# Grouped queries' root on GpSimd, the last heads' sums added through a 0/1 column, weight transfers queued at their buffer's due time

## The chip, the cores and the metric

One core of a Trainium2 chip runs the whole kernel. The metric is device time in microseconds (us): the median of the runs, 1585.17 for the kernel before (three runs, 1583.2 to 1587.08). Engines are called PE (TensorE matmuls), PEld (its weight loads), DVE (VectorE), ACT (ScalarE), POOL (GpSimd) and SP (SyncE, which only issues transfers here).

## The reference

Two layers of an encoder trunk over 512 tokens of width 1024, all in float32:

```python
h = rms_norm(x, attn_norm_g[l])
proj = h @ w_in[l]
c_q, c_kv, k_rope, gq, gk, gv, pool_in, gate_logits = split_columns(proj, IN_SIZES)
o_mla = mla_branch(c_q, c_kv, k_rope, ...)      # 8 heads, low-rank q and kv
o_gqa = gqa_branch(gq, gk, gv, ...)             # 8 query heads, 2 key heads, 64 wide
o_pool = pool_branch(pool_in, pool_w[l], pool_scale[l])
gates = sigmoid(gate_logits)                    # one per branch and channel
merged = sum(gate * (o @ w_branch) for the three branches)
x = x + merged @ w_out[l]
x = x + (silu(u_gate) * u_val) @ ffn_w_down[l]  # u: depthwise conv of rms_norm(x) @ ffn_w_up
```

In the grouped branch each of the 8 query heads is scaled by one over the root of its mean square plus 1e-6. For 512 tokens and 8 heads that is 128 x 32 numbers on the chip.

## The kernel before, in words

Float32 products are made of three matmuls of split operands (`mm3`, L382): each weight tile and each activation is cut into a rounded part and a remainder. The weights stream through a pool of three raw buffers (`rawp`, `RAW = 3`), each 1024 columns wide as a rule and filled by one transfer on SP (`w_dma`, L326). A buffer holds about two pieces of up to 512 columns. `w_split` (L333) cuts a piece: ACT writes the rounded part `wh`, then POOL or DVE subtracts it to give `wl`; `pick` decides which. Pieces are cut `LA = 3` ahead of the matmul that uses them.

The order on every engine is written by a planner inside the kernel: a `Clock` keeps an estimated time for each engine, `chain` queues the steps of a tile's way through the engines at their estimated times, and every PSUM bank has an estimated time at which it is free. Matmuls are emitted one after another, and what is due by the estimate is emitted ahead of them. The hardware then runs each engine's list in that order and waits on semaphores; an engine that waits holds up all that stands behind it.

A layer runs in this order. The normed input is multiplied with the latent columns, the pooled channels (four groups), the grouped queries (banks `AV`, `AV`, `mi`, `ST`) and the grouped keys and values; in the middle of the last stands the pooled branch's own product (`pool_product`). It uses the same four banks as the queries, and each bank is free again when DVE has made the remainder `opl` of that bank. Then come the gates of branch 2, whose first two take the `AV` banks, and the attention of the grouped heads.

The root of the grouped queries is stepped by hand: `gq_mean` scales and adds epsilon, `guess` makes a first value from the bits, three Newton steps follow, and `gq_token` multiplies with the token's own factor. All of it works on `ssr`, 128 x 32. `rsqrt_steps` (L440) makes these steps; without an engine given it puts all of them on DVE, nine instructions in three Newton steps. Four multiplications `gq_norm` on POOL follow, and the queries are then turned by PE (L379) or through DRAM.

Attention (`attention`) writes a list of steps for eight heads with positions `PLAN`: scores for the maximum (`s_max`, bank `S`), scores for the probabilities (`probs`, banks `ST`, `ST`, `mi`), products with the values (`av_hi`, `av_lo`), and a last product that adds a remainder (`av_rest`). The tiles `ph`, `pl` and `vt` carry the rounded probabilities, their remainder and that last sum. Between these steps a `Filler` puts units of other matmuls (gates, the branch products, the making of the latent heads' q, k, v): as many as the position asks for, and up to `SLACK = 35` more when the planner believes the step would wait. What is left of the filler when the last step is out goes behind it; the filler of the next attention starts after that. The latent heads' values leave their bank `acc` by a cast and four DVE subtractions (`vm`).

At a head pair's end (`o_out`, L1311) the two halves `oraw` and the row `osum` of sums have been copied from PSUM. Rows 0 and 64 of `osum` hold the sum of probabilities; the other rows hold remainders that have to be added to `oraw`. So, after a transpose and a reciprocal have taken what they need, `add` sets rows 0 and 64 to zero by two POOL memsets and adds the tiles: on POOL, and for head 7 on DVE.

The lines that matter: `w_ahead` (L357) queues weight transfers, `rsqrt_steps` (L440), `gq_mean` and `gq_token` in `layer`, `add` in `o_out`, and the memsets at the start (L1565).

Of the kernel before, what the change touches and what calls it, by code (L numbers as in the profile page):

```python
# [18 lines left out]
P = 128  # L19
T = 512  # L20
# [112 lines left out]
class Clock:  # L133
# [10 lines left out]
    def at(self, dt, fn):  # L144
        heapq.heappush(self.heap, (self.now + dt, self.n, fn))
        self.n += 1
# [24 lines left out]
    def done(self, *key):  # L171
        self.ready[key] = self.fin + self.SEM
# [90 lines left out]
def trunk(ctx: ExitStack, tc: tile.TileContext, x, w, prm, gb, cst, out):  # L263
# [62 lines left out]
    def w_dma():  # L326
        i = st["dma"]
        t = slot("raw") if i < KC else rawp.tile([P, 1024], F32, tag="raw", name=f"raw{i}")
        SY.dma_start(t[:, :swidth[i]], w[int(soff[i]):int(soff[i + 1])].rearrange("(p c) -> p c", p=P))
        raws[i] = t  # L330
        st["dma"] += 1

    def w_split():  # L333
        j = st["split"]
        sl, off, wd = pieces[j]
        r = raws[sl][:, off:off + wd]
        hi = hlp.tile([P, T], F32R, tag="wh", name=f"wh{j}")
        lo = hlp.tile([P, T], F32R, tag="wl", name=f"wl{j}")
        ck.fin = ck.now
        if j == 0:  # L340
            V.tensor_copy(hi[:, :wd], r)
        else:
            A.activation(hi[:, :wd], r, AF.Copy)
        e = V if j < KC + 3 else pick(W_BIAS, ck.fin + ck.SEM)
        ck.free[e.kind] = max(ck.free.get(e.kind, 0.0), ck.fin + ck.SEM)
        e.tensor_tensor(lo[:, :wd], r, f(hi[:, :wd]), ALU.subtract)
        done("w", j)
        halves[j] = (hi, lo)
        st["split"] += 1

    def pick(bias, t=0.0):

# [1 line left out]
        dve, pool = (max(t, ck.free.get(e, 0.0)) for e in ("DVE", "Pool"))  # L354
        return V if dve + 0.61 + bias < pool + 1.18 else G

    def w_ahead(j):  # L357
        while True:
            sj = st["split"]
            done = pieces[sj][0] if sj < len(pieces) else len(swidth)  # L360
            while st["dma"] < min(len(swidth), done + RAW):
                w_dma()
            if sj > min(j, len(pieces) - 1):
                return
            w_split()

    def wnext():
# [26 lines left out]
    xsp = dp.tile([KC, P, T], F32, tag="xsp", name="xsp")  # L394
    ident = C[:, C_ID:C_ID + P]
    mhalf = cp.tile([P, 1], F32, tag="mhalf", name="mhalf")
    eps = cp.tile([P, 1], F32, tag="eps", name="eps")


    MQ, MK = [[cp.tile([P, 4, 4, 96], F32, tag=f"{n}{g}", name=f"{n}{g}") for g in range(2)] for n in ("MQ", "MK")]  # L400
# [39 lines left out]
    def rsqrt_steps(a, n, key, eng=None):  # L440

        if n == 8:
            return [lambda: G.tensor_tensor(a, a, bc(mhalf, [P, 8]), ALU.pow), lambda: done(*key)]
        y = small("y0", [P, 32])[:, :n]
        t = small("yt", [P, 32])[:, :n]

        def newton(to):
            if eng:
                eng.tensor_tensor(t, y, a, ALU.mult)
                eng.tensor_tensor(t, t, y, ALU.mult)  # L450
                eng.tensor_scalar(t, t, -0.5, 1.5, ALU.mult, ALU.add)
                eng.tensor_tensor(to, t, y, ALU.mult)
                return
            V.tensor_tensor(t, y, a, ALU.mult)
            V.scalar_tensor_tensor(t, t, -0.5, y, ALU.mult, ALU.mult)
            V.scalar_tensor_tensor(to, t, 1.5, y, ALU.add, ALU.mult)

        def guess():
            V.tensor_scalar(y.bitcast(I32), a.bitcast(I32), -0.5, RSQRT_BITS, ALU.mult, ALU.add)

        def go():
            guess()
            for to in (y, y, a):
                newton(to)

        if eng:
            return [guess, *[lambda to=to: newton(to) for to in (y, y, a)], lambda: done(*key)]
        return [go, lambda: done(*key)]

    def norm_begin(gen, sq):  # L470

# [45 lines left out]
    def bc(ap, shape):  # L517
        return ap.to_broadcast(shape)
# [26 lines left out]
    def layer(l, sq, xsrc):  # L545
# [226 lines left out]
            chain(add, lambda: done("gqr", l, b), after=ck.fin - ck.now)  # L772

        def gq_mean():
            V.scalar_tensor_tensor(ssr[:, 0:32], ssr[:, 0:32], 1.0 / 64, bc(eps, [P, 32]), ALU.mult, ALU.add)

        def gq_token():
            s_ = ssr[:, 0:32].rearrange("p (b h) -> p b h", b=4)
            V.tensor_tensor(s_, s_, bc(nrm["rt"].unsqueeze(2), [P, 4, 8]), ALU.mult)

        def gq_norm(b):
            o = gqo[b][:, :T].rearrange("p (h f) -> p h f", f=64)
# [2 lines left out]

        chain(*[lambda b=b: gq_square(b) for b in range(4)])
        chain(*[lambda b=b: gq_rope(b) for b in range(4)])
        chain(([("gqs", l, b) for b in range(4)], gq_mean), *rsqrt_steps(ssr[:, 0:32], 32, ("ssr", l)), gq_token,
              *[([("gqr", l, b), ("gkn", l)], lambda b=b: gq_norm(b)) for b in range(4)])

        opool = {}
# [344 lines left out]
        def attention(kind, fill, okey, odst):  # L1136
# [174 lines left out]
            def o_out(h):  # L1311
                s = hs.pop(h)
                if h % 2 == 0:
                    ot[:] = [slot("oraw"), slot("osum")]
                raw, sums = ot
                js = slice(64 * (h % 2), 64 * (h % 2) + 64)

                def in_order(o, src):
                    if not gqa or h > 1:
                        o = o.rearrange("p (b i t) -> p i b t", b=4, i=4)  # L1320
                        src = src.rearrange("p (i b t) -> p i b t", b=4, i=4)
                    A.activation(o, src, AF.Copy)

                def copies():
                    in_order(sums[js, :T], s["av"][64:128])
                    in_order(raw[js, :T], s["av"][0:64])
                    free("AV")

                def add():

                    for j in (0, 64):
                        G.memset(sums[j:j + 1, :T], 0.0)
                    (V if h == 7 else G).tensor_tensor(raw[:, :T], raw[:, :T], sums[:, :T], ALU.add)

                steps = [copies]
                if h % 2 == 1:
                    oh, ol = slot("oh", F32R), slot("ol", F32R)
                    odst[h // 2] = (oh, ol)

                    turned, inv = slot("otr"), small("oinv", [P, 16])  # L1340
                    steps += [lambda: V.transpose(turned[:, :T], sums[:, :T]),
                              lambda: V.reciprocal(inv, turned[:, :T].rearrange("p (b f) -> p b f", f=32)[:, :, 0])]
                    steps += [add, lambda: (A.activation(inv[32:64], inv[0:32], AF.Copy),
                                            A.activation(inv[96:128], inv[64:96], AF.Copy))]
                    steps += [lambda: V.transpose(sums[:, :T].rearrange("p (b f) -> p b f", f=32),
                                                  bc(inv.unsqueeze(2), [P, 16, 32]))]
                    steps += [lambda: (V if h == 7 else G).tensor_tensor(raw[:, :T], raw[:, :T], sums[:, :T], ALU.mult),
                              *split(oh[:, :T], ol[:, :T], raw[:, :T], eng=V if h == 7 else G),
                              lambda: done(okey, l, h // 2)]
                chain(*steps)  # L1350
# [211 lines left out]
    V.memset(warm, 0.0)  # L1562
    A.activation(warm, warm, AF.Exp)
    V.memset(mhalf, -0.5)
    V.memset(eps, EPS)  # L1565
    G.memset(f(unit), 0.0)
    G.memset(f(unit[:, 0:1]), 1.0)
    idle = ps("mi")
# [169 lines left out]
```

## Time and profile before

| what | value |
|---|---|
| median of the runs (range) | 1585.17 us (1583.2 to 1587.08) |
| the profiled execution's own span, first instruction to last | 1584.1 us |
| mean granted PE clock | 0.997 |
| PE busy | 1567.5 us, 99% |
| DVE, ACT, POOL busy | 949.1, 789.7, 1022.0 us |
| weight transfers of 512 KB on SP | 230, median 3.4 us to landing |

The span is within the range of the timed runs and 1.07 us under their median. A view of waits gives, for an engine, the line that waited, who released it, the total in us, how often, and the longest. A timeline gives the start, the busy time, engine, line, operation, output and inputs, and in brackets the idle time before it with its releaser. A table by stretches gives the busy time of each engine with its number of instructions, the granted clock, the share of the transfer engines and GB/s. A row on a tile gives the least, the median and the largest duration in ns.

### The profile page before, as it was taken

Reading aid. Unit: us, or ns where it says so; the run is one execution under the profiler, and the core shown is the slowest. Engines: PE = TensorE matmul, PEld = TensorE weight load, DVE = VectorE, ACT = ScalarE, POOL = GpSimd, SP = SyncE. Lnnn points to the kernel's source line nnn. Section 1 sums busy time; section 2 is a strip of 40 time slices with the busy share of each in tenths; the row PEclk is TensorE's granted clock in tenths of the full one; section 3 lists DMA queues with packets and bytes.
Section 4 is the critical chain, followed back from the end, with each engine's and each line's share of the span. In section 5 each row is a group of like instructions: output and inputs, shape, how many; then the busy total and the mean of one; then the engine's idle time right before and its main releaser. Section 6 shows DMA issues by size and latency. Waiting matters only on the chain.

```text
span 1584.1 us, 20341 instructions
## 1 busy us (share of the span) xinstructions
PE 1567.5 (99%) x7098; PEld 1310.2 (83%) x7098; DVE 949.1 (60%) x1351; ACT 789.7 (50%) x1436; POOL 1022.0 (65%) x889
## 2 busy tenths in 40 slices
PE   9989999999999999999999999999999999999999
PEld 8878878888888888888898888788888888888888
DVE  6767876875257776720047788678652677777000
ACT  5547766763444444432244677666634444444221
POOL 3854886754667667654568658868546676666542
PEclk9999999999999999999999999999999999999999
DMA  6422224323323232233335322343242233223331
GB/s 206 125 92 81 77 82 146 117 67 120 120 80 107 93 107 93 94 120 107 113 107 129 103 72 74 101 142 103 67 146 93 83 108 103 94 93 106 120 113 47
DMA packets 86070, 164.43 MB, mean 104 GB/s; under 512 B 25040, under 2 KB 47056, under 8 KB 85968
## 3 DMA queue, kind: packets, MB, share of 16 engines
q1 hardware_dynamic: 81072, 162.93, 32.5%
q8 instruction: 56, 0.92, 0.2%
q10 hardware_dynamic: 4896, 0.21, 0.2%
q14 instruction: 46, 0.38, 0.1%
HBM read 149.41 MB, written 13.63 MB: 103 GB/s over the span
## 4 chain that ended last, share of the span: by engine, by line
PE 90%; DVE 4%; POOL 2%; DMA 1%; ACT 1%; issue 1%; SPq 0%; ACTq 0%; POOLq 0%; DVEq 0%
PE ps_acc L375 40%; PE ps_AV L375 22%; PE ps_ST L375 21%; PE ps_S L375 3%; PE ps_mi L375 3%; DVE XM L231 1%; DMA raw<-w 1%; POOL wl L231 1%; DVE mgl L231 1%; ACT mgh L224 1%; DVE gt L235 0%; POOL win L231 0%; POOL tabm L231 0%; POOL fac L231 0%; DMA tf<-dl 0%
## 5 line engine op out<-in xcount | busy, mean ns | idle before, releaser
L231 POOL TENSOR_TENSOR wl<-raw,wh 128x512 fp32r<-128x512 f32 (+2 forms) x502 | 675.4, 1357 | 420.0 <-ACT wh L224 388.5
L224 ACT ACTIVATE wh<-raw 128x512 fp32r<-128x512 f32 (+3 forms) x521 | 308.8, 606 | 124.5 <-PE ps_ST L375 45.5
L235 DVE SCALAR_TENSOR_TENSOR a<-u,prm,a 128x511 f32<-128x511 f32 x176 | 241.6, 1375 | 90.8 <-ACT a L224 87.8
L375 PE MATMUL ps_acc<-HH,wh 128*128 128x512 f32 x592 | 232.2, 392 | 6.0 <-DVE vm L231 5.7
L375 PE MATMUL ps_acc<-HL,wh 128*128 128x512 f32 x592 | 231.8, 392 | 0.0
L375 PE MATMUL ps_acc<-HH,wl 128*128 128x512 f32 x592 | 231.8, 392 | 0.0
L375 PEld LDWEIGHTS ps_acc<-HH,wh 128*128 128x128 f32 x592 | 111.7, 189 | 29.1 <-issue 7.1
L375 PEld LDWEIGHTS ps_acc<-HH,wl 128*128 128x128 f32 x592 | 111.6, 188 | 23.9
L375 PEld LDWEIGHTS ps_acc<-HL,wh 128*128 128x128 f32 x592 | 111.6, 188 | 22.9
L375 PE MATMUL ps_AV<-HH,wh 128*128 128x512 f32 x288 | 113.7, 395 | 4.7 <-DVE ssr L231 4.2
L375 PE MATMUL ps_AV<-HL,wh 128*128 128x512 f32 x288 | 113.2, 393 | 0.0
L375 PE MATMUL ps_AV<-HH,wl 128*128 128x512 f32 x288 | 113.1, 393 | 0.0
L231 POOL TENSOR_TENSOR al<-a,ah 128x512 fp32r<-128x512 f32 x44 | 58.1, 1320 | 83.4 <-ACT ah L224 81.4
L239 DVE TENSOR_REDUCE nm<-ps_S 128x1 fp32r<-128x512 f32 x128 | 87.6, 684 | 33.0 <-PE ps_S L375 31.8
L375 PE MATMUL ps_ST<-HH,wh 128*128 128x512 f32 x240 | 93.5, 390 | 0.0
L375 PE MATMUL ps_ST<-HL,wh 128*128 128x512 f32 x240 | 93.4, 389 | 0.0
L375 PE MATMUL ps_ST<-HH,wl 128*128 128x512 f32 x240 | 93.4, 389 | 0.0
L224 ACT ACTIVATE ah<-a 128x512 fp32r<-128x512 f32 x44 | 27.8, 632 | 127.8 <-DVE a L231 127.8
L224 ACT ACTIVATE a<-u,prm 128x512 f32<-128x512 f32 x88 | 71.0, 809 | 24.8 <-DVE u L231 24.4
L224 ACT ACTIVATE a<-a 128x512 f32<-128x512 f32 x44 | 27.6, 632 | 103.4 <-DVE a L235 103.4
L224 ACT ACTIVATE HH<-XM,prm 128x512 fp32r<-128x512 f32 x32 | 23.1, 722 | 103.6 <-DVE XM L231 53.9
L224 ACT ACTIVATE ps_ST<-ps_ST 128x512 f32<-128x512 f32 x86 | 49.9, 581 | 49.3 <-PE ps_ST L375 49.3
(376 smaller groups left out, 3727.1 us busy)
## 6 DMA issues: line engine op xcount, KB each, us to landing
raw<-w SPq DMA_DIRECT2D x230, 512.0 KB, 3.4
raw<-w SPq DMA_DIRECT2D x14, 384.0 KB, 3.1
XM<-x SPq DMA_DIRECT2D x16, 256.0 KB, 3.6
dtq<-tr SPq DMA_DIRECT2D x16, 192.0 KB, 3.0
dtk<-tr SPq DMA_DIRECT2D x16, 192.0 KB, 3.6
tf<-dtq SPq DMA_DIRECT2D x48, 64.0 KB, 2.1
tf<-dtk SPq DMA_DIRECT2D x48, 64.0 KB, 2.3
xsp<-XM SPq DMA_DIRECT2D x8, 256.0 KB, 2.0
```

Of the source, the lines that this page charges most:

```text
L224: return self.eng.activation(out, in_, func, **k)
L231: return self.eng.tensor_tensor(out, *a)
L235: return self.eng.scalar_tensor_tensor(out, *a)
L239: return self.eng.tensor_reduce(out, in_, *a, **k)
L375: PE.matmul(o, lhsT=lhsT, rhs=rhs, start=start, stop=stop)
```

## The change

There are three edits. **The root:** `gq_mean`, the Newton steps and `gq_token` of the grouped queries go to POOL; only `guess` stays on DVE. A Newton step is now four POOL instructions in place of three on DVE, and the planner puts each step out by itself. **The sums:** for head 7, `add` no longer has POOL set rows 0 and 64 to zero: one DVE instruction multiplies `osum` with a column `keep` (1, with 0 in rows 0 and 64) and adds `oraw`. `keep` takes the place of `eps` and is made by three memsets at the start. **The transfers:** the transfer that refills a buffer was queued on SP in the same call that had split the last piece out of it; now it is queued when, by the planner's clock, that split is done. What is due before then goes ahead of it on SP.

```diff
@@ w_split
         st["split"] += 1
+        if j + 1 == len(pieces) or pieces[j + 1][0] > sl:
+            at(ck.fin - ck.now, lambda: w_until(sl + RAW))
...
+    def w_until(i):
+        while st["dma"] <= min(i, len(swidth) - 1):
+            w_dma()
+
     def w_ahead(j):
-        while True:
-            sj = st["split"]
-            done = pieces[sj][0] if sj < len(pieces) else len(swidth)
-            while st["dma"] < min(len(swidth), done + RAW):
-                w_dma()
-            if sj > min(j, len(pieces) - 1):
-                return
+        while st["split"] <= min(j, len(pieces) - 1):
+            w_until(pieces[st["split"]][0])
             w_split()
...
-    eps = cp.tile([P, 1], F32, tag="eps", name="eps")
+    keep = cp.tile([P, 1], F32, tag="keep", name="keep")
...
         def newton(to):
-            if eng:
-                eng.tensor_tensor(t, y, a, ALU.mult)
-                eng.tensor_tensor(t, t, y, ALU.mult)
-                eng.tensor_scalar(t, t, -0.5, 1.5, ALU.mult, ALU.add)
-                eng.tensor_tensor(to, t, y, ALU.mult)
-                return
-            V.tensor_tensor(t, y, a, ALU.mult)
-            V.scalar_tensor_tensor(t, t, -0.5, y, ALU.mult, ALU.mult)
-            V.scalar_tensor_tensor(to, t, 1.5, y, ALU.add, ALU.mult)
+            eng.tensor_tensor(t, y, a, ALU.mult)
+            eng.tensor_tensor(t, t, y, ALU.mult)
+            eng.tensor_scalar(t, t, -0.5, 1.5, ALU.mult, ALU.add)
+            eng.tensor_tensor(to, t, y, ALU.mult)
...
-        def go():
-            guess()
-            for to in (y, y, a):
-                newton(to)
-
-        if eng:
-            return [guess, *[lambda to=to: newton(to) for to in (y, y, a)], lambda: done(*key)]
-        return [go, lambda: done(*key)]
+        return [guess, *[lambda to=to: newton(to) for to in (y, y, a)], lambda: done(*key)]
...
         def gq_mean():
-            V.scalar_tensor_tensor(ssr[:, 0:32], ssr[:, 0:32], 1.0 / 64, bc(eps, [P, 32]), ALU.mult, ALU.add)
+            G.tensor_scalar(ssr[:, 0:32], ssr[:, 0:32], 1.0 / 64, EPS, ALU.mult, ALU.add)
...
-            V.tensor_tensor(s_, s_, bc(nrm["rt"].unsqueeze(2), [P, 4, 8]), ALU.mult)
+            G.tensor_tensor(s_, s_, bc(nrm["rt"].unsqueeze(2), [P, 4, 8]), ALU.mult)
...
-        chain(([("gqs", l, b) for b in range(4)], gq_mean), *rsqrt_steps(ssr[:, 0:32], 32, ("ssr", l)), gq_token,
+        chain(([("gqs", l, b) for b in range(4)], gq_mean), *rsqrt_steps(ssr[:, 0:32], 32, ("ssr", l), G), gq_token,
...
                 def add():
 
+                    if h == 7:
+                        V.scalar_tensor_tensor(raw[:, :T], sums[:, :T], keep, raw[:, :T], ALU.mult, ALU.add)
+                        return
                     for j in (0, 64):
                         G.memset(sums[j:j + 1, :T], 0.0)
-                    (V if h == 7 else G).tensor_tensor(raw[:, :T], raw[:, :T], sums[:, :T], ALU.add)
+                    G.tensor_tensor(raw[:, :T], raw[:, :T], sums[:, :T], ALU.add)
...
-    V.memset(eps, EPS)
+    V.memset(keep, 1.0)
+    for j in (0, 64):
+        V.memset(keep[j:j + 1], 0.0)
```

The planner estimates with the new costs, so the order moves in more places than the diff names. Three of them follow. The first is DVE's list in layer 0, from the last of the queries' rotations (`rp`, `gqr`) on; `ssr`, `y` and `yt` are the root, `opl` the remainders that free the banks. Before:

```order
L231 TENSOR_TENSOR gqr_799<-ps_ST_581,tabg_155 128x512
L235 SCALAR_TENSOR_TENSOR ssr_342<-ssr_342,eps 128x32
L243 TENSOR_SCALAR y_102_800<-ssr_342 128x32
L231 TENSOR_TENSOR yt_801<-y_102_800,ssr_342 128x32
L235 SCALAR_TENSOR_TENSOR yt_801<-yt_801,y_102_800 128x32
L235 SCALAR_TENSOR_TENSOR y_102_800<-yt_801,y_102_800 128x32
...
L235 SCALAR_TENSOR_TENSOR ssr_342<-yt_801,y_102_800 128x32
L235 SCALAR_TENSOR_TENSOR opl_944<-ps_AV_928,prm_92,oph_943 128x512
L231 TENSOR_TENSOR ssr_342<-ssr_342,rt_397 128x32
L235 SCALAR_TENSOR_TENSOR opl_951<-ps_AV_945,prm_92,oph_950 128x512
```

The same place in the change:

```order
L231 TENSOR_TENSOR gqr_801<-ps_ST_583,tabg_157 128x512
L235 SCALAR_TENSOR_TENSOR opl_934<-ps_AV_926,prm_92,oph_933 128x512
L235 SCALAR_TENSOR_TENSOR opl_941<-ps_AV_935,prm_92,oph_940 128x512
L243 TENSOR_SCALAR y_102_802<-ssr_344 128x32
L235 SCALAR_TENSOR_TENSOR opl_949<-ps_mi_942,prm_92,oph_948 128x512
L235 SCALAR_TENSOR_TENSOR opl_958<-ps_ST_950,prm_92,oph_957 128x512
```

Eleven instructions of the root that stood ahead of the first `opl` are gone from DVE, and `guess` (`y`) stands behind the second. The second place is POOL's list in the same stretch of the change, where before only the `wl` and `gqr` rows stood (`wl_960` and `wl_985` belong to the first gate):

```order
L243 TENSOR_SCALAR ssr_344<-ssr_344 128x32
L231 TENSOR_TENSOR wl_923<-raw_790,wh_922 128x288
L231 TENSOR_TENSOR gqr_801<-gqr_801,rp_115_906 128x512
L231 TENSOR_TENSOR wl_960<-raw_860,wh_959 128x512
L231 TENSOR_TENSOR yt_803<-y_102_802,ssr_344 128x32
L231 TENSOR_TENSOR yt_803<-yt_803,y_102_802 128x32
L243 TENSOR_SCALAR yt_803<-yt_803 128x32
L231 TENSOR_TENSOR y_102_802<-yt_803,y_102_802 128x32
L231 TENSOR_TENSOR wl_985<-raw_860,wh_984 128x512
```

The Newton steps now stand between the weight splits, and the PE transposes of the queries, which need the root, stand at PE's row 490 of the program and no longer at 469: 21 filler matmuls have moved ahead of them. The third place is PE's list at the end of the grouped attention in layer 0, at the last scores of head 7 (`ST_2488` before, `ST_2516` in the change); `acc` rows are filler. Before, from row 989 on:

```order
L375 MATMUL ps_ST_2488<-qa_2027,ka_589 128x512
L375 MATMUL ps_ST_2488<-qb_2028,kb_590 128x512
L375 MATMUL ps_acc_2446<-HH,wh_2318 128x512
L375 MATMUL ps_acc_2446<-HL,wh_2318 128x512
L375 MATMUL ps_acc_2446<-HH,wl_2319 128x512
L375 MATMUL ps_AV_2466<-ph_2425,vg_584 128x512
L375 MATMUL ps_acc_2446<-HH,wh_2369 128x512
L375 MATMUL ps_acc_2446<-HL,wh_2369 128x512
L375 MATMUL ps_acc_2446<-HH,wl_2370 128x512
L375 MATMUL ps_AV_2343<-pl_2356,vg_586 128x512
```

The last product of the attention (`vt`) stands at row 1009. In the change that product stands at row 1009 too, but the last scores only at row 998:

```order
L376 MATMUL ps_ST_2516<-qa_2104,ka_591 128x512
L376 MATMUL ps_ST_2516<-qb_2105,kb_592 128x512
L376 MATMUL ps_AV_2512<-ph_2493,vg_586 128x512
L376 MATMUL ps_AV_2430<-pl_2447,vg_588 128x512
L376 MATMUL ps_AV_2430<-vt_2385,unit 128x512
L376 MATMUL ps_AV_2512<-ph_2510,vg_587 128x512
L376 MATMUL ps_AV_2512<-pl_2483,vg_585 128x512
L376 MATMUL ps_AV_2512<-ph_2521,vg_588 128x512
L376 MATMUL ps_AV_2512<-pl_2494,vg_586 128x512
L376 MATMUL ps_AV_2512<-pl_2511,vg_587 128x512
L376 MATMUL ps_AV_2512<-pl_2522,vg_588 128x512
L376 MATMUL ps_AV_2512<-vt_2502,unit 128x512
```

From row 986 to row 1009 the change has no filler: the grouped attention's share of it is used up at row 985, where before nine filler matmuls stood between row 991 and row 1001. The second layer has the same rows, 3507 further down.

## The prediction

> **What bounds the kernel now.** I read the page first, then who makes PE wait, then the timelines at the longest waits.
>
> ```profile
> PE 1567.5 (99%) x7098; PEld 1310.2 (83%) x7098; DVE 949.1 (60%) x1351; ACT 789.7 (50%) x1436; POOL 1022.0 (65%) x889
> ...
> PE 90%; DVE 4%; POOL 2%; DMA 1%; ACT 1%; issue 1%; SPq 0%; ACTq 0%; POOLq 0%; DVEq 0%
> ```
>
> PE is busy for 1567.5 of 1584.1 us, and the chain that ends last is PE for 90%. No edit changes a matmul. So the change can gain only where PE waits or runs slowly, and it loses only where PE comes to wait. PE's waits by releaser:
>
> ```profile
> PE ps_acc L375 <- DVE vm L231: 5.7, 2, 2.9
> PE ps_AV L375 <- DVE ssr L231: 4.2, 1, 4.2
> PE ps_mi L1570 <- DVE eps L259: 1.0, 1, 1.0
> PE ps_AV L375 <- ACT gkn L224: 0.5, 1, 0.5
> ```
>
> Two rows tower: 4.2 us once, in layer 0, and 2.9 us in each layer. Each also leaves something behind, which the table by stretches shows (duration first, then PE's busy time with its matmuls; granted clock third from the end):
>
> ```profile
> 86.70:92.93 6.23, 6.22 (x15) 4.93 (x16) 6.11 (x17) 0.00 (x0) 2.14 (x2) 0.52 0.01 2
> 398.50:404.00 5.50, 5.50 (x25) 4.51 (x25) 1.45 (x3) 2.29 (x4) 4.16 (x4) 1.00 0.54 182
> 1017.50:1021.26 3.76, 3.72 (x10) 2.94 (x10) 2.63 (x5) 0.63 (x1) 0.30 (x3) 0.55 0.92 256
> 234.30:240.80 6.50, 6.43 (x30) 5.14 (x30) 4.90 (x12) 3.48 (x7) 0.81 (x4) 1.00 0.88 243
> ```
>
> At full clock 25 matmuls take 5.50 us, 0.22 each. After the 4.2 us wait the clock is 0.52 and 15 take 6.22, so 2.9 us more are lost; after the wait at 1017 ten take 3.72, 1.5 lost; after the same wait at 234 the clock stayed at 1.00. The waits thus cost 4.2 + 5.7 + 2.9 + 1.5 = 14.3 us.
>
> **The root.** DVE's timeline before the 4.2 us wait:
>
> ```profile
> 76.02 0.95 DVE L235 SCALAR_TENSOR_TENSOR ssr<-ssr,eps 128x32 f32<-128x32 f32 x1
> ...
> 85.82 0.74 DVE L235 SCALAR_TENSOR_TENSOR opl<-ps_AV,prm,oph 128x512 fp32r<-128x512 f32 x1
> ```
>
> The root holds DVE from 76.02 to 85.82, and the first `opl`, which frees the bank of the first gate, stands behind it in the list; PE goes on at 86.71. In the change `opl` stands ahead of all of it, right after the rotations, and can end near 78, before PE arrives at about 82.5 (86.71 less the wait). What is late next? The gate needs its first `wl`. POOL's rows:
>
> ```profile
> L231 POOL TENSOR_TENSOR yt<-y,ssm x12: 242/250/264, 166.5 to 989.5; 128x32 f32<-128x32 f32 x12
> L231 POOL TENSOR_TENSOR yt<-yt,y x12: 250/253/256, 166.8 to 989.8; 128x32 f32<-128x32 f32 x12
> L243 POOL TENSOR_SCALAR yt<-yt x12: 216/217/221, 167.1 to 990.1; 128x32 f32<-128x32 f32 x12
> ```
>
> ```profile
> 78.89 1.28 POOL L231 TENSOR_TENSOR wl<-raw,wh 128x512 fp32r<-128x512 f32 x1
> ```
>
> The latent root makes the same steps on POOL, so the new cost is known: three Newton steps of 3 x 0.25 + 0.22, and 0.22 and 0.25 at the ends, 3.4 us in a layer. The first gate's `wl` ran at 78.89; behind 0.22 of `gq_mean` it ends at 80.4, 2 us before PE needs it. The second piece stands behind one Newton step (0.97), so it ends at 80.4 + 0.97 + 1.28 = 82.7, and is needed 12 matmuls after 82.5, at 85.1. Both are covered. So 4.2 + 2.9 goes, and the 0.5 of layer 1, where the first `opl` also comes behind the root.
>
> The queries are ready later on POOL; PE's transposes need them:
>
> ```profile
> 105.55 0.60 PE L379 MATMUL ps_mi<-C,gqr 128*128 128x128 f32 x4
> ```
>
> ```profile
> 101.42 1.05 POOL L231 TENSOR_TENSOR gqr<-gqr,ssr 128x512 f32<-128x512 f32 x1
> ...
> 103.50 3.78 POOL L231 TENSOR_TENSOR wl<-raw,wh 128x512 fp32r<-128x512 f32 x3 [1.02 <-ACT wh L224]
> ```
>
> Before, the last product ended at 102.5, 3.1 us ahead. In the change two more `wl` stand before it: on the old clock they would end at 106.0 (103.50 and two of three 1.26), it at 107.1. All that follows PE comes 7.1 us sooner, so 100. The transposes come 7.1 sooner and 21 filler matmuls later (nine full, twelve of 384 columns, some 4 us), so at 102.5. That leaves 2.5 us of cover. If the root took longer than that, PE would wait there.
>
> A page of the Trainium skill speaks against this edit: "GPSIMD Engine Reference", section "4.1 Engine selection", sends elementwise work to VectorE, GpSimd being about twice as slow for two inputs. By it the 9.8 us of DVE would be some 20 on POOL, an estimate from that page and the timeline; the rows of 0.25 us say otherwise for tiles this small, and the sum goes by them.
>
> **The sums.** DVE before the wait at 234, and PE:
>
> ```profile
> 231.07 0.69 DVE L231 TENSOR_TENSOR oraw<-oraw,osum 128x512 f32<-128x512 f32 x1 [4.87 <-POOL osum L259]
> 231.68 1.75 DVE L231 TENSOR_TENSOR wl<-raw,wh 128x512 fp32r<-128x512 f32 x1
> 233.35 0.87 DVE L231 TENSOR_TENSOR vm<-ps_acc,vm 128x252 fp32r<-128x252 f32 x4
> ```
>
> ```profile
> 234.37 0.47 PE L375 MATMUL ps_acc<-HH,wh 128*128 128x512 f32 x1 [2.87 <-DVE vm L231]
> ```
>
> DVE stands 4.87 us before head 7's addition because POOL's two memsets come late in POOL's list; behind it wait a `wl` and the `vm` that free the bank. Without memsets DVE has nothing to wait for. The new instruction lies between 0.69 (this addition) and 1.75 us (the `wl`, also two inputs, while POOL ran); I take 0.69, its own size. At the high end 1 us of the 4.87 comes back, still enough. So 5.7 + 1.5 goes. After the latent heads the same edit shortens no wait of PE.
>
> **The transfers.** SP's waits:
>
> ```profile
> SPq L329 <- POOL wl L231: 1108.3, 236, 10.3
> ...
> SPq L1123 <- DMA dtq<-tr: 24.0, 10, 4.4
> ```
>
> A weight transfer leaves when its buffer is free, and PE never waited for one; a later place in the list changes that only where small transfers now stand ahead and themselves wait, 2.4 us each (24.0 over 10). A transfer lands in a median 3.4 us and its buffer is wanted two buffers later, four pieces of 12 matmuls: 4 x 2.6 = 10.6 us. The 7 us between hide 2.4. The latents' transfers leave sooner, and PE waits for none. I take zero; the ends are 10 x 2.4 = 24 us a cost, if nothing hid it, and no gain.
>
> **What the new order costs.** The 21 filler matmuls that went ahead of the transposes are missing at the end of the grouped attention. Before, the last scores and the product at its end:
>
> ```profile
> 219.19 0.40 PE L375 MATMUL ps_ST<-qb,kb 65*128 65x512 f32 x1
> ...
> 223.57 0.39 PE L375 MATMUL ps_AV<-vt,unit 128*128 128x512 f32 x1
> ```
>
> That was 4.4 us with 19 rows between, and no wait. In the change it is ten rows, 10 x 0.22 = 2.2 us. What has to happen in them:
>
> ```profile
> L224 ACT ACTIVATE ps_ST<-ps_ST 128x512 f32<-128x512 f32 x86 | 49.9, 581 | 49.3 <-PE ps_ST L375 49.3
> L224 ACT ACTIVATE ph<-ps_ST 128x512 fp32r<-128x512 f32 x60 | 35.6, 593 | 1.5
> ...
> L224 ACT ACTIVATE oinv<-oinv 32x16 f32<-32x16 f32 x32 | 6.8, 214 | 0.6
> ```
>
> ```profile
> L247 DVE CAST ph<-ps_ST 128x512 fp32r<-128x512 f32 x26 | 17.8, 686 | 8.4 <-ACT ps_ST L224 8.2
> ```
>
> ```profile
> L235 DVE SCALAR_TENSOR_TENSOR vt<-ps_ST,vg,vt x32: 703/741/743, 126.3 to 1005.7; 128x512 fp32r<-128x512 f32 x32
> ...
> L224 ACT ACTIVATE vt<-ps_ST,vg x12: 672/683/691, 122.5 to 998.1; 128x512 fp32r<-128x512 f32 x12
> ```
>
> After the last scores (0.40) come the exponential 0.58, the cast 0.69, and on DVE `vt`, `pl`, `vt` of 0.74, 0.68 (the cast's size) and 0.74: 3.8 us, so PE waits at least 1.6. From head 7's first scores on, PE has 22 rows, 4.9 us, without filler. ACT has in the same piece four exponentials, three casts, a `vt` and two small copies of some 0.2, 5.2 us, with 0.4 before and DVE's 2.8 behind: 8.4, a wait of 3.5. No gain is possible here, as there was no wait. I take 3.0, nearer to the fuller list: 6.0 in both layers.
>
> **The sum.** 14.3 + 0.5 - 6.0 = 8.8: 1584.1 becomes 1575.3 for the profiled execution. It lies 1.07 under the median of the runs, so I forecast **1576.4 us**.
>
> **The rivals.** (1) *The new waits slow the clock.* A wait of 2.87 us did so at 1017 and did not at 234; if each new one costs 2.9 as at 86, the time is 1576.4 + 5.8 = 1582.2. Against it: the new wait falls into pieces with matmuls between. The Trainium skill, "TensorE: Matmul & The Clock Gate", section "HAM oscillation — how this bites in real kernels", names idle gaps over some 3.4 us as what throttles; by it this rival would never come. The trace does not agree, as 2.87 us was enough at 1017, so it keeps its chance: 0.17. (2) *The edit doesn't do what it says:* the bank is free, but the gate waits for `wl` behind the Newton steps. If the whole 4.2 + 2.9 stays: 1583.5. The 2 us of cover speaks against it: 0.08. (3) *Slower: the root on POOL.* If its 14 instructions took 1.28 each beside the weight splits, as a full one does, they would take 18 and not 3.4 us; 14.5 more, less the cover of 2.5, is a wait of 12 in each layer: 1576.4 + 24 = 1600. It turns slower than before from 2.5 + 8.8 / 2 = 6.9 us more per layer on. The rows of 0.25 speak against it: 0.08. (4) *No new wait at the end of the attention:* 1570.4; 0.07. The forecast has 0.60.
>
> **How the numbers follow.** About 0.2% (3.2 us) is what a measurement here can tell from no change, so faster means under 1582.0. The forecast, (4) and half of (1) lie there: 0.76. Half of (1) and (2): 0.16. Slower: 0.08. The range goes from (4) to just past (2), 1570 to 1584; the ends of the new wait (1.6 and 3.5) and slow clock in one layer lie inside, and 0.08 is left out.
>
> **What would show it.** Right: no wait of PE on `ssr`, none on `vm`, clock 1.00 near 85 and 1010, and a new wait of PE on ACT or DVE at `ps_ST` and `ps_AV` ahead of the last `vt`, some 3 us per layer. Wrong: PE waiting on POOL's `wl` near 82, on `gqr` near 102, or on a `raw` transfer.

## The result, and the profile after

The changed kernel took **1584.02 us** (median of 19 runs, 1583.29 to 1586.22) against 1586.15 for the kernel before in the same comparison: a ratio of 0.999, 95% interval 0.9984 to 0.9997. That is 2.1 us faster, inside the 0.2% that I had called no change; I had forecast 8.8 us. The profiled execution went from 1584.1 to 1581.9 us.

First the page: PE's busy time, and the chain that ended last.

```profile
span 1581.9 us, 20358 instructions
...
PE 1567.1 (99%) x7098; PEld 1308.3 (83%) x7098; DVE 946.0 (60%) x1335; ACT 790.7 (50%) x1440; POOL 1023.1 (65%) x901
...
PE 91%; DVE 4%; ACT 2%; DMA 1%; issue 1%; POOL 0%; SPq 0%; ACTq 0%; DVEq 0%
```

PE's waits in the change (total, how often, the longest):

```profile
PE ps_acc L376 <- DVE vm L231: 2.9, 2, 1.5
PE ps_ST L376 <- ACT vt L224: 2.5, 2, 1.3
PE ps_AV L376 <- DVE ph L247: 1.7, 2, 0.9
...
PE ps_AV L376 <- DVE pl L231: 0.6, 2, 0.3
PE ps_S L376 <- DVE nm L239: 0.6, 2, 0.3
```

The wait of 4.2 on `ssr` is gone, and every wait left is shorter than 1.6 us. The two on `vm` are not those of before: they stand at 205.66 and 991.49 us, inside the grouped attention. The stretches that were slow before now run at full clock: in the first, 28 matmuls begin in 6.23 us (the row's 30 counts two that began just before), where before it was 15:

```profile
82.70:88.93 6.23, 6.23 (x30) 5.13 (x29) 5.60 (x9) 3.85 (x13) 5.98 (x8) 1.00 0.49 155
1009.60:1015.10 5.50, 5.50 (x29) 4.65 (x28) 4.44 (x7) 4.41 (x9) 3.17 (x5) 1.00 0.42 135
1015.10:1021.00 5.90, 5.90 (x31) 4.98 (x30) 4.50 (x12) 3.92 (x8) 3.42 (x5) 1.00 0.42 109
```

DVE's timeline shows the root's edit at work: two `opl` right behind the rotations, ended at 78.25, and PE takes the bank at 82.70.

```profile
76.07 0.67 DVE L231 TENSOR_TENSOR gqr<-ps_ST,tabg 128x512 f32<-128x512 f32 x1
76.81 1.44 DVE L235 SCALAR_TENSOR_TENSOR opl<-ps_AV,prm,oph 128x512 fp32r<-128x512 f32 x2
78.17 0.33 DVE L243 TENSOR_SCALAR y<-ssr 128x32 int32<-128x32 int32 x1
```

POOL's timeline, with the first gate's `wl` and the queries' last product, and the transposes on PE:

```profile
79.68 1.29 POOL L231 TENSOR_TENSOR wl<-raw,wh 128x512 fp32r<-128x512 f32 x1
80.94 0.72 POOL L231 TENSOR_TENSOR yt<-y,ssr 128x32 f32<-128x32 f32 x1
...
99.20 2.54 POOL L231 TENSOR_TENSOR wl<-raw,wh 128x512 fp32r<-128x512 f32 x2
101.71 1.04 POOL L231 TENSOR_TENSOR gqr<-gqr,ssr 128x512 f32<-128x512 f32 x1
```

```profile
102.84 0.60 PE L380 MATMUL ps_mi<-C,gqr 128*128 128x128 f32 x4
```

The `wl` ended at 80.97 (I had 80.4). The last product ended at 102.75, not at 100, so of the 2.5 us of cover 0.1 were left; it was enough. The loss is at the end of the grouped attention. PE from head 7's last scores on, with the idle time and its releaser in brackets:

```profile
218.60 0.51 PE L376 MATMUL ps_ST<-qa,ka 128*128 128x512 f32 x1 [1.26 <-ACT vt L224]
218.94 0.40 PE L376 MATMUL ps_ST<-qb,kb 65*128 65x512 f32 x1
...
221.39 0.50 PE L376 MATMUL ps_AV<-ph,vg 128*128 128x512 f32 x1 [0.87 <-DVE ph L247]
221.73 0.63 PE L376 MATMUL ps_AV<-pl,vg 128*128 128x512 f32 x2
222.65 0.50 PE L376 MATMUL ps_AV<-pl,vg 128*128 128x512 f32 x1 [0.29 <-DVE pl L231]
223.31 0.51 PE L376 MATMUL ps_AV<-vt,unit 128*128 128x512 f32 x1 [0.16 <-DVE vt L235]
```

That is the forecast wait, at the forecast place, with idle times of 1.26 + 0.87 + 0.29 + 0.16 = 2.6 us and some 0.2 of start behind each, 3.4 in all. But it isn't alone. Thirteen us earlier PE waits on `vm`, which stands behind a weight split on DVE:

```profile
205.66 0.47 PE L376 MATMUL ps_acc<-HH,wh 128*128 128x512 f32 x1 [1.45 <-DVE vm L231]
```

```profile
202.48 1.59 DVE L231 TENSOR_TENSOR wl<-raw,wh 128x512 fp32r<-128x512 f32 x1
203.99 0.74 DVE L235 SCALAR_TENSOR_TENSOR vt<-ps_mi,vg,vt 128x512 fp32r<-128x512 f32 x1
204.65 0.87 DVE L231 TENSOR_TENSOR vm<-ps_acc,vm 128x252 fp32r<-128x252 f32 x4
```

The next table holds the start of marked PE rows, in us, for before, the change and three experiments told below (sums alone; Newton steps in one piece; filler held back). It shows where time is won and lost.

| PE row | before | change | sums alone | in one piece | held back |
|---|---|---|---|---|---|
| layer 0, first gate | 86.71 | 82.70 | 86.69 | 82.58 | 82.50 |
| transposes of the queries | 105.55 | 102.84 | 104.28 | 98.54 | 102.63 |
| last product of the grouped attention | 223.57 | 223.31 | 222.30 | 216.67 | 219.36 |
| first product `vt` of the latent heads | 267.93 | 264.43 | 263.21 | 257.58 | 260.27 |
| layer 1, first gate | 872.26 | 867.77 | 869.19 | 860.92 | 863.62 |
| last product of the grouped attention | 1006.74 | 1009.14 | 1003.28 | 995.02 | 1001.46 |
| first product `vt` of the latent heads | 1052.40 | 1050.18 | 1044.19 | 1035.93 | 1042.37 |
| end of the span | 1584.12 | 1581.94 | 1575.95 | 1567.69 | 1574.16 |

From the first gate to the last product of the grouped attention PE has the same work in all five. The change takes 140.6 us for it in layer 0 and 141.4 in layer 1; the kernel in one piece takes 134.1 in both. PE sits idle for 4.3 and 4.8 us of the change's time there and for none in the kernel in one piece; the rest of the difference, 2.2 and 2.5 us, was not broken down beyond the slow starts behind the waits.

### The profile page after: what moved, and what is told of

It reads as the page before. It is cut to its first block, busy times and chain, and to the rows that moved or that the text cites. A ratio compares the mean times of both kernels' runs of the same rounds, so it can differ in the third digit from the quotient of the medians.

```text
span 1581.9 us, 20358 instructions
## 1 busy us (share of the span) xinstructions
PE 1567.1 (99%) x7098; PEld 1308.3 (83%) x7098; DVE 946.0 (60%) x1335; ACT 790.7 (50%) x1440; POOL 1023.1 (65%) x901
## 4 chain that ended last, share of the span: by engine, by line
PE 91%; DVE 4%; ACT 2%; DMA 1%; issue 1%; POOL 0%; SPq 0%; ACTq 0%; DVEq 0%
PE ps_acc L376 40%; PE ps_AV L376 22%; PE ps_ST L376 22%; PE ps_S L376 4%; PE ps_mi L376 3%; DVE XM L231 1%; DVE mgl L231 1%; ACT mgh L224 1%; DMA XM<-x 1%; DVE gt L235 0%; DVE sq L231 0%; DMA raw<-w 0%; ACT wh L224 0%; DVE vt L235 0%; ACT ph L224 0%
## 5 line engine op out<-in xcount | busy, mean ns | idle before, releaser
L231 POOL TENSOR_TENSOR wl<-raw,wh 128x512 fp32r<-128x512 f32 (+3 forms) x494 | 668.3, 1364 | 397.5 <-ACT wh L224 377.3
```

The costliest lines, as they stand in the source:

```text
L231: return self.eng.tensor_tensor(out, *a)
```

## The experiments

Theory A: the root's edit delays the queries in the planner's time, the planner runs five more units (21 matmuls) of filler ahead of the transposes, and that filler is missing later, at more places than the one I had priced. Its rivals put the loss on the other two edits, on POOL's load, or on the late transposes themselves. Each ratio is against the kernel before on the same chip.

**The root alone.**

```
-            V.scalar_tensor_tensor(ssr[:, 0:32], ssr[:, 0:32], 1.0 / 64, bc(eps, [P, 32]), ALU.mult, ALU.add)
+            G.tensor_scalar(ssr[:, 0:32], ssr[:, 0:32], 1.0 / 64, EPS, ALU.mult, ALU.add)
...
-            V.tensor_tensor(s_, s_, bc(nrm["rt"].unsqueeze(2), [P, 4, 8]), ALU.mult)
+            G.tensor_tensor(s_, s_, bc(nrm["rt"].unsqueeze(2), [P, 4, 8]), ALU.mult)
...
-        chain(..., *rsqrt_steps(ssr[:, 0:32], 32, ("ssr", l)), gq_token,
+        chain(..., *rsqrt_steps(ssr[:, 0:32], 32, ("ssr", l), G), gq_token,
```

> The kernel before with the first edit alone (root on POOL, stepped). Theory A: the root's edit alone moves the 21 filler matmuls ahead of the transposes, and their lack at the end of the grouped attention costs about 6.5 us in each layer. Then the root's gain of 4.2 + 2.9 + 0.5 = 7.6 is lost again: 7.6 - 13.4, and the two waits on vm stay, so about 5.8 us slower than before. PE waits in the profile: none on ssr, two on vm near 230 and 1013 of 2.9, and waits on vt and ph near 218 to 224 and 1004 to 1010. Rival B: the loss in the grouped attention comes from the sums or from the transfers' place on SP; then this kernel is 7.6 us faster than before and has no waits at 218.

Measured: 1584.94 us against 1584.62, ratio 1.0001 (0.9992 to 1.001). PE's waits in this kernel:

```profile
PE ps_acc L375 <- DVE vm L231: 2.9, 2, 1.5
PE ps_ST L375 <- ACT vt L224: 2.5, 2, 1.3
PE ps_AV L375 <- DVE ph L247: 1.8, 2, 0.9
PE ps_acc L375 <- DVE gt L231: 1.2, 2, 0.6
```

The late waits are there, so this edit brings them by itself and rival B falls. But I had expected 5.8 us slower. The two long waits on `vm` near 234 and 1017, which I had left in the sum, are gone without the sums' edit; 0.6 us on `gt` are left at each place. POOL's memsets start sooner, at 227.31 and not at 229.95 (POOL's timelines, this kernel and before), because less of POOL's other work is left between head 6's addition and them (two products on `MK`, the latent heads' keys, have gone ahead); so DVE waits 2.09 us and not 4.87:

```profile
227.31 1.09 POOL L259 MEMSET osum<- 1x512 f32 x2
```

```profile
229.95 1.09 POOL L259 MEMSET osum<- 1x512 f32 x2
```

```profile
228.43 0.69 DVE L231 TENSOR_TENSOR oraw<-oraw,osum 128x512 f32<-128x512 f32 x1 [2.09 <-POOL osum L259]
```

PE is at the last product at 223.58, no sooner than before: the work that went ahead left waits there and took this one away. That is why the change has so little of the sums' gain left: 1.7 us between the two spans, 1583.6 and 1581.9.

**Three kernels with a tile too many.** The next three were first built with the column `keep` beside `eps`, not in its place. The short diffs, on the kernel before (the first) and on the change (the others):

```
+    keep = cp.tile([P, 1], F32, tag="keep", name="keep")
...
+                    if h == 7:
+                        V.scalar_tensor_tensor(raw[:, :T], sums[:, :T], keep, raw[:, :T], ALU.mult, ALU.add)
+                        return
```

```
-        while not ck.has(*[("gqn", l, b) for b in range(4)]) and fa.step():
+        while not ck.has(*[("gqn", l, b) for b in range(4)]) and fa.done < 22 and fa.step():
...
-                        return [("gqn", l, b) for b in range(4)], "mi"
+                        return [], "mi"
```

```
+        if key[0] == "ssr":
+            return [guess, lambda: [newton(to) for to in (y, y, a)], lambda: done(*key)]
         return [guess, *[lambda to=to: newton(to) for to in (y, y, a)], lambda: done(*key)]
```

> The kernel before with the second edit alone (0/1 column). Theory A: the two waits on vm of 2.9 us and the slow clock after the second (1.5) go, nothing else moves: 7.3 us faster than before. PE waits 4.2 on ssr in layer 0 as before, and there is no wait on vt or ph near 218. Rival B: the longer DVE instruction, or what follows it on DVE, brings the waits at 205 and 218; then the gain is eaten and the time is within 2 us of before, or above it.

> The changed kernel, with the filler ahead of the grouped attention held to the 22 units that the kernel before puts there (the change puts 27), so that the transposes stand at their old row; the lists of POOL, with the root's steps between the splits, stay those of the change. Theory A: the waits at 205 and 218 to 224 go, 13.4 us in both layers; but the last product of the queries ends at about 102.75 as in the change, while the transposes are reached at about 98.7, so PE waits 4.1 us on gqr in each layer: about 5 us faster than the change, or, if the clock slows by 2.9 after each such wait, about the same as the change. Rival B: the root's load on POOL among the splits brings the late waits, whatever the order on PE; then they stay and the new wait comes on top, 8 us slower than the change.

> The changed kernel, with the three Newton steps of the grouped queries' root handed to the planner as one piece, so that all twelve POOL instructions stand together and three splits fewer stand ahead of the queries' last product. The planner then puts the transposes at their old row by itself. Theory A: the last product ends near 99 (102.75 less three splits of 1.27), the transposes come near 98.7 and wait under 0.5, and the attention's end has its filler again: 13 us faster than the change, about 1571. Rival B: the root's load on POOL brings the late waits: same as the change within 2 us. Rival C: the gate's second wl now stands behind all three Newton steps, two more of 0.97, and PE waits for it near 85: of the 13 us, some 1 to 2 in each layer are lost.

Measured: 1594.67 (ratio 1.0058, 1.0046 to 1.0071), 1598.01 (1.0078, 1.0064 to 1.0092) and 1591.95 (1.0043, 1.003 to 1.0055). No time fits its theory A, and only the first fits its rival, which left room for anything above before. But the late waits were gone in all three, as the theories had it, so the lost time lay elsewhere. The stretches told where, since in the feed-forward part, where PE waits for nothing, fewer matmuls fit into the same time at a clock of 1.00. Before, and the first of the three:

```profile
500.00:600.00 100.00, 100.00 (x443) 82.81 (x442) 72.14 (x65) 44.32 (x74) 68.98 (x47) 1.00 0.31 100
```

```profile
500.00:600.00 100.00, 100.00 (x430) 80.60 (x429) 68.14 (x63) 43.87 (x71) 62.41 (x46) 1.00 0.28 96
```

The work there is the same in both; what I suspected was the place of the tiles behind the added column. So all three were built again with `keep` in the place of `eps`, as in the change (all three then have 443 matmuls in this stretch, as before), and the suspicion was tested by itself:

```
     eps = cp.tile([P, 1], F32, tag="eps", name="eps")
+    pad = cp.tile([P, 1], F32, tag="pad", name="pad")
...
+    V.memset(pad, 1.0)
```

> The kernel before with one more column of 128 x 1 behind eps, set once and never read, so that the tiles behind it move by 32 bytes. Theory A': the matmuls that read weights as their moving operand take 0.233 and no longer 0.227 us each; 7.0 us in each feed-forward part and about 1.6 elsewhere, 15.6 us slower than before. Rival (the places do not matter): same as before within 1 us.

Measured: 1602.76 against 1584.02, ratio 1.0114 (1.0101 to 1.0127), 18.7 us slower for a column that nobody reads. The stretch has 430 matmuls like the three kernels, 0.233 us each and not 0.226:

```profile
500.00:600.00 100.00, 100.00 (x430) 80.60 (x429) 69.47 (x62) 43.75 (x72) 64.04 (x45) 1.00 0.28 95
```

**The sums alone, again.**

> The second edit alone again, but with the column keep in the place of eps, as in the change, so that no tile moves in SBUF (the earlier kernel kept both columns, and 32 bytes more stood ahead of all that follows them); the mean is then a scalar instruction on DVE with epsilon as a constant. Theory A': the 3% slower matmuls of the feed-forward part in the three earlier kernels came from the tiles' places, not from the edits. Outside of that part the first kernel with the sums alone stood 3.6 us ahead of before at the end of layer 0's attention and gained 3.2 in layer 1's: about 7 us faster than before here, 1577.7. Rival: the slow matmuls belong to the order of the work; then about 1594 again.

Measured: 1576.97 against 1584.02, ratio 0.9954 (0.9939 to 0.9968): 7.05 us faster than before, and some 5 faster than the whole change (7.05 less its 2.1, each against the kernel before beside it). PE still waits on the root, and on nothing late in the attention:

```profile
PE ps_AV L375 <- DVE ssr L231: 6.2, 2, 4.2
```

**The transposes at their old row, again.**

> The change with the filler held to 22 units ahead of the grouped attention, made from the change itself so that no tile moves. Theory A': 3.9 us ahead of before at the end of layer 0's attention, and 0.7 lost in layer 1's (PE waits 3.5 us in all on gqr), about 3 us faster than before. Rival (the slow matmuls come from the order): about 1598 again.

Measured: 1580.02, ratio 0.9968 (0.9956 to 0.998), 4.0 us faster than before. With the filler of before the late waits are gone, though up to the queries' last product POOL's list is that of the change, so the root's load on POOL by itself isn't their cause. The price is a wait for the queries themselves, 1.7 us in layer 0 and 2.6 in layer 1:

```profile
PE ps_mi L380 <- POOL gqr L231: 4.3, 2, 2.6
```

So the planner had a reason: the queries are late on POOL, and PE pays either at the transposes or at the end.

**The Newton steps in one piece, again.**

> The change with the three Newton steps put out as one piece, made from the change itself so that no tile moves. Theory A': 6.3 us ahead of before at the end of layer 0's attention and 3.1 more in layer 1's, 9.4 us faster than before, about 1575, and 7 faster than the change. Rival (the slow matmuls come from the order): about 1592 again.

Measured: **1569.38 us**, ratio 0.9904 (0.9891 to 0.9917), 14.6 us faster than before and the fastest kernel here. Its only difference from the change is that the planner can put nothing between the three steps. POOL then has five splits, not eight, between the gate's first and the last product, which ends at 98.87; the transposes are back at their old row, at 98.54:

```profile
97.83 1.04 POOL L231 TENSOR_TENSOR gqr<-gqr,ssr 128x512 f32<-128x512 f32 x1
```

```profile
98.54 0.71 PE L380 MATMUL ps_mi<-C,gqr 128*128 128x128 f32 x4
```

What PE still waits for, in all 1567.7 us, lies outside of the attention:

```profile
PE ps_mi L1566 <- DVE keep L259: 1.1, 1, 1.1
PE ps_S L376 <- DVE prt L239: 0.8, 1, 0.8
PE ps_acc L376 <- DVE mgl L231: 0.5, 2, 0.2
```

**The filler held back.** The late order stays, but in the grouped attention the filler may run only 10 units ahead of its plan:

```
+            SL = 10 if gqa else SLACK
             f0, first = fill.done, plan[0][0]
...
-                while fill.done < target + SLACK and waiting(fn, *args) and fill.step():
+                while fill.done < target + SL and waiting(fn, *args) and fill.step():
```

> The change as it is, transposes at the late row and root stepped on POOL, but in the grouped attention the filler may run at most 10 units ahead of its plan, not 35 (the latent attention keeps 35). At the last scores of head 7 there are then again 19 rows to the end with the filler of before. Theory A: the waits at 205 and at 218 to 224, 5.2 us in each layer, come from the filler used up too soon, so about 10 us faster than the change, 1574; what is held back may open small waits earlier, up to some 2 us. Rival: the late transposes themselves delay the heads, and the waits move to another place of the attention; then within 2 us of the change, 1582 to 1584.

Measured: 1576.59 against 1585.49, ratio 0.9951 (0.9939 to 0.9964). The waits at 205 and 218 are gone with the transposes still late, so the late transposes don't bring these by themselves. But the rival is half right: the kernel still lies 6.5 us above the one in one piece by the spans (1574.2 - 1567.7), of the 14.3 that the change lies above it. Whether the late order or the held filler costs these 6.5 was not tested apart. In their place stand waits on `XM` (the sum that the layer carries on) of 3.2 us in all, two of 1.4 at 156 and 938 and one of 0.4 that the change has too, and small ones on `MK`:

```profile
PE ps_acc L376 <- DVE XM L235: 3.2, 3, 1.4
PE ps_acc L376 <- ACT MK L224: 1.2, 2, 0.6
```

**The transfers alone.** The third edit as in the change, on the kernel before.

> The kernel before with the third edit alone. The prediction took zero. Theory A: same as before within 1 us, and the same four waits of PE. Rival: the transfers queued later reach their splits late; PE then waits on a split of wl or wh and the time is 2 us or more above before.

Measured: ratio 1.0004 (0.9995 to 1.0013), 1586.02 against 1585.49, the span 1584.1 as before, and the same long waits. The edit is worth nothing that can be measured.

**Nine columns more.** As with one column, with a width of 9 in place of 1, so 64 bytes and not 32.

> The kernel before with a tile of 128 x 9 behind eps, set once and never read, so that the tiles behind it move by 64 bytes instead of 32. Theory: only the place modulo 64 bytes counts, so same as before, with 0.227 us a matmul in the feed-forward part. Rival: any move of the tiles slows it; then about 1600 as with one column.

Measured: 1602.55, ratio 1.0112 (1.0098 to 1.0126). My guess of 64 bytes is wrong; which distance would be harmless was not tried.

**Stepped on DVE.** In the change, `G` put back to `V` at the three places of the first diff (the mean keeps its form).

> The change with the root left on DVE but stepped, each Newton step four DVE instructions; the first opl stands behind two of the three steps, and PE's list is that of the sums alone, transposes at their old row. Theory: a small DVE instruction takes 1.2 us while POOL is at work, so ten of them before the first opl are as long as the whole root before; PE waits about 4 in layer 0, and the time is that of the sums alone, 1577. Rival: what helped was putting the steps out apart, not POOL; then the wait on the first opl is gone or under 1 us, and the time is near 1569 as with the steps in one piece on POOL.

Measured: 1574.09, ratio 0.9935 (0.9922 to 0.9949), between theory and rival. The steps beside POOL's splits are as slow as expected, those in a pause of POOL are not, and the first `opl` stands behind them:

```profile
79.19 1.22 DVE L231 TENSOR_TENSOR yt<-yt,y 128x32 f32<-128x32 f32 x1
...
84.16 0.19 DVE L231 TENSOR_TENSOR yt<-yt,y 128x32 f32<-128x32 f32 x1
84.39 0.18 DVE L243 TENSOR_SCALAR yt<-yt 128x32 f32<-128x32 f32 x1
84.61 0.19 DVE L231 TENSOR_TENSOR y<-yt,y 128x32 f32<-128x32 f32 x1
84.72 0.75 DVE L235 SCALAR_TENSOR_TENSOR opl<-ps_AV,prm,oph 128x512 fp32r<-128x512 f32 x1
```

```profile
85.61 0.47 PE L376 MATMUL ps_AV<-HH,wh 128*128 128x512 f32 x1 [2.92 <-ACT krt L224]
```

The `opl` ends at 85.47 and PE goes on at 85.61 after a wait of 2.92, not 4.2 (the view names ACT's `krt`, which ends at 85.58; the bank is freed by `opl`). The clock stayed at 1.00 behind it in this execution, and layer 1 didn't wait. So the rival has a part: putting the steps out apart lets one Newton step less stand ahead of `opl`. By the ratios it is worth some 3 us over the sums alone (0.9954 to 0.9935), and the root on POOL in one piece some 5 more (0.9935 to 0.9904), 2.9 of which is the wait that is left.

## Why the prediction was wrong

- **What bounds the kernel: right.** Waits of PE, and the slow clock behind them, were what could be won. The kernel in one piece has none of the long waits and no slow clock, and is 14.6 us faster than before; I had 14.8 to win.
- **The root: right.** 4.2 + 2.9 + 0.5 = 7.6. One piece against the sums alone, in one comparison: 1576.97 - 1569.38 = 7.6. That the figures agree so well is in part luck: in the profile of the sums alone the slow clock costs 1.5 us and not 2.9 (135.6 - 134.1 by the table), and layer 1 waits 2.0 us on the root and not 0.5. The cover of the gate's first `wl` held.
- **The sums: right, with one value off.** Forecast 7.2, measured 7.05 alone (5 to 10 by the interval). The new instruction takes 0.68 us in that kernel and 1.61 in the change, where I took 0.69 between 0.69 and 1.75. What I missed is that the gain isn't added to the root's: in the order that the root's edit brings, the memsets come sooner and most of the wait for them is gone already.
- **The transfers: right**, zero.
- **The step that failed: what the new order costs.** "I take 3.0, nearer to the fuller list: 6.0 in both layers." The change lies 14.3 us above the kernel in one piece by the spans (1581.9 - 1567.7), and 12.5 by the times, each against the kernel before beside it (14.6 - 2.1). By the table it is 140.6 - 134.1 = 6.5 us in layer 0 and 141.4 - 134.1 = 7.3 in layer 1. So the term of 6.0 measures 13.8, or 12.5 by the times, and of the 6.7 us that the gain fell short (8.8 - 2.1) it makes 6.5. The tail that I had worked out step by step measures 3.4, close to the 3.5 of the fuller list. The rest I didn't look for: 1.6 at 205 and 991, 0.4 at 883, small ones near 161 and 947, and what the table leaves open. I had priced the last 22 rows of the attention and taken all rows ahead of them as unchanged. They are filled from the same stock: filler that is spent early is missing, or differently placed, in the whole stage.
- **The queries' arrival: wrong, 2.75 us too early.** I moved POOL's old clock 7.1 us forward with PE and added two splits. In the change POOL's timeline marks no wait from 74.43 to 102.75, so its own load and not PE sets the arrival. Of splits it has eight between the gate's first and the last product, where before it had seven: three more pieces are cut there, and DVE takes two of them. The root takes 5.3 us in layer 0 and not 3.4. So the planner's late turn was not caution but just enough, by 0.1 us.
- **The offset.** I set the median 1.07 us above the span. Before's median with more runs was 1586.15 and not 1585.17, and the change's lies 2.1 above its span; each single run lies 1.7 to 2.2 above its own span. This makes about 1 us of the 7.6 between forecast and result; the failed step makes nearly all of the rest.
- **The rivals.** New waits slowing the clock: not here, each is under 1.6 us and the clock in those stretches is 1.00. The root as long as a split on POOL: no, though its small steps took up to 0.72 and not 0.25 us while DVE was at work. A wait at the gate: none.

Shown is that the root's edit alone brings the late waits, that either the filler's old share (with the transposes at their old row) or holding it back removes them, and that letting splits in between the Newton steps is what made the planner move it. Not shown is what of the late order's cost is the filler's lack and what the late turn itself, since holding the filler back wins about half. Only argued is how 1.6 us at 205 come about: the split of 1.59 on DVE stands ahead of `vm` there, and no run took away that split alone.

## What to carry to other kernels

When a short dependent chain moves to an engine that also does bulk work, put it out in one piece: between single steps a scheduler lets that engine's long instructions in, and the chain's last step is late by all of them (here three splits, which turned 14.6 us of gain into 2.1). When an order moves filler forward, price the whole stage that shares the stock, not the place where it runs out. And compare variants with every tile at its old place: here one unread column cost more than any edit brought.

## What the runs showed of the hardware

**The place of a tile.** One or nine unread columns ahead of the weight tiles (32 or 64 bytes by my count; no view shows addresses) made the feed-forward matmuls take 0.233 and not 0.226 us, at a clock of 1.00 and with no wait in the stretch. The whole kernels took 18.7 and 17.1 us more. What in the chip does it is open.

**The clock after a wait.** The table by stretches, right behind a wait, in five experiments (transfers alone, sums alone, one column more, stepped on DVE, transposes at their old row again):

```profile
234.67:240.67 6.00, 6.00 (x22) 5.08 (x23) 4.15 (x9) 3.95 (x7) 2.17 (x6) 0.72 0.69 240
```

```profile
869.19:874.19 5.00, 5.00 (x22) 4.15 (x23) 4.96 (x12) 1.76 (x8) 2.22 (x2) 1.00 0.30 98
```

```profile
85.45:91.45 6.00, 6.00 (x19) 4.78 (x20) 5.96 (x17) 1.59 (x7) 3.15 (x3) 0.72 0.22 78
```

```profile
85.61:91.61 6.00, 6.00 (x27) 4.96 (x28) 5.86 (x16) 0.82 (x3) 1.05 (x2) 1.00 0.19 70
```

```profile
31.32:36.32 5.00, 5.00 (x16) 4.01 (x17) 1.51 (x4) 0.00 (x0) 4.14 (x2) 0.66 0.02 9
```

The same wait of 2.9 us near 234 left the clock at 1.00 in the kernel before (the prediction's row) and at 0.72 with the transfers alone. A wait of 2.0 (sums alone, layer 1) left it at 1.00, one of 2.2 (one column more) at 0.72, one of 2.9 (stepped on DVE) at 1.00. The shortest wait that slowed it is that of the last row, 1.63 us; waits of 1.5 in the change left it at 1.00. The Trainium skill, "TensorE: Matmul & The Clock Gate", section "HAM oscillation — how this bites in real kernels", names gaps over some 3.4 us; these runs show slowing behind waits of 1.63 to 4.2 us, in some executions and not in others.

**Small DVE instructions beside POOL.** On 128 x 32 the same instruction takes 1.22 us while POOL is at its splits and 0.19 in POOL's pause (the rows of 79.19 and 84.16 above).
